# A trunk layer's first projections on unnormed x, with the rows' factor applied behind them

## The chip, the cores and the metric

The kernel runs on one core of one Trainium2 chip. The metric is device time in microseconds, the median of three runs. Five engines work side by side, each in the order in which the program gives it its instructions: TensorE (PE, with its weight loads as PEld), VectorE (DVE), ScalarE (ACT), GpSimd (POOL) and SyncE (SP), which here only issues transfers. An engine waits on semaphores for what another one or a DMA has to deliver; whatever stands behind the waiting instruction on the same engine waits too.

## The reference

One decoder layer on x of 512 rows and 1024 columns, all float32. Only the beginning matters here:

```python
u = rmsnorm(x, ln1_g[i])          # x * rsqrt(mean(x*x) + eps) * g
proj = u @ w_in[i]
q, k, v, pool_in, z, xbc, dt_raw, gate_pre = jnp.split(proj, split_idx, axis=-1)
...
y_a = dilated_attention_mixer(q, k, v, rel_bias) @ w_a[i]
y_b = pool_mixer(pool_in, pool_w[i], pool_scale[i]) @ w_b[i]
y_c = ssd_mixer(z, xbc, dt_raw, ...) @ w_c[i]
...
x = x + merged @ w_o[i]
x = x + conv_ffn(rmsnorm(x, ln2_g[i]), ...)
return rmsnorm(x, final_g)
```

The norm's factor is one number for each row of x; `g` is one for each column. So a projection of `x * g` differs from that of `u` by a factor for each row of the output. `pool_mixer` takes windowed means of 2, 4, 8 and 16 rows of `pool_in`, less `pool_in` itself, and multiplies by small matrices. The attention has three groups of heads, and their values `v` are three stretches of 384 columns.

## The kernel before

**Products in three parts.** A float32 matrix is split in a high part (the value rounded to the fast float32 format of PE) and a low part (what is left). `mm3` (line 230) makes each product from three: high by high, high by low, low by high. So every operand costs a copy to the high part (mostly ACT) and a subtraction for the low one (mostly DVE).

**Jobs.** `program` (line 1709) yields the jobs in order: four jobs for `pool_in` (256 columns each, two PSUM results of 128 columns by 512 rows), two for the first value group (400 columns with `dt_raw`, four K blocks each, four blocks of rows), three for q and k, then `pool_out_job`, and so on. A job's weights are fetched by SP (`fetch`, line 173) to one of two raw buffers, cast to the high part by ACT (`cast`, line 185) and subtracted by DVE to the low part (`low`, line 221). The loop at line 1943 stands ahead of each job's products with the low part of the next job, the cast of the one after and the fetch of the third.

**Small work between.** `step` (line 155) advances what is in `running` and `waiting` by one segment, mostly once for each PSUM result. `after(n, it)` holds a generator back by n steps. The queue of each engine is in program order (`ORDERED`, line 1975), so where `step` is called sets what stands behind what.

**The start.** Lines 1797 to 1939 load x in eight tiles of 128 rows by 512 columns, and `eye` and the gains `g8`. For row blocks 0 and 1 the sums of squares, a root and a few small operations give each row's factor, which goes on the diagonal of `diag`; `turn_scale` (line 1875) multiplies by it, so a transposed and normed block comes out in one product. `turned` (line 1844) applies `g` and splits, 256 columns at a time, to `uh` and `ul`, the transposed normed x in eight blocks of K. Blocks 2 and 3 are scaled in place and transposed (`turns`). `begin` (line 1851) issues the products of the first two jobs in two halves of 256 rows; its last calls evacuate with `pool_evac`. `WARM` products at the start keep PE busy before data is there.

**Pooling.** `pool_evac` (line 890) copies the PSUM result to `pu` on ACT, adds it up in windows on POOL (a doubling sum `psw`: one addition for windows of 2, four for 16, each with a small copy for the first columns), and two steps later DVE and ACT form `pd` and its parts.

**Values and sums.** `v_jobs` (line 621) evacuates by ACT copies to `v0` and `dtr`. `sums_of_u` (line 402) rebuilds u as `uh + ul` in pairs of blocks and makes the sums that `Seven` (line 346), a scheme with seven products in place of eight, needs later. `v_pair` (line 641) makes value groups 1 and 2 that way; its `done` issues the transfers of the rows to their places from SP as soon as the instruction that forms them is written.

**Memory.** Most tiles of 128 by 512 come from one pool of `NBIG` = 52 (`T`, line 106). PSUM has four banks for products (`MM`) and four for small work (`SM`).

Of the kernel before, what the change touches and what calls it, by code (L numbers as in the profile page):

```python
# [82 lines left out]
def trunk(ctx: ExitStack, tc, out, x, rel_bias, ln1_g, w_in, b_gate, w_a, pool_w, pool_scale, w_b,  # L83
# [318 lines left out]
    def sums_of_u(p):  # L402

        f = []
        for k in (2 * p, 2 * p + 1):
            f.append(T("uf"))
            dve.tensor_tensor(f[-1], uh[:, k, :].bitcast(F32), ul[:, k, :].bitcast(F32), OP.add)
# [208 lines left out]
    dtr = cpool.tile([P, 4, SH], F32, name="dtr")  # L616

    both = cpool.tile([P, 4, 32 + HEADS], F32, name="nmls")
    V, QK, OT, NM, LS = {}, {}, {}, {}, {}

    def v_jobs(g):
# [16 lines left out]
        return jobs_b(parts, 384 + extra, lambda k, tb: uh[:, k, tb * P:(tb + 1) * P],  # L638
                      lambda k, tb: ul[:, k, tb * P:(tb + 1) * P], KD, evac)

    def v_pair():
# [9 lines left out]
        def done(hi, right, i, r, ps, op):  # L651
# [10 lines left out]
            for n in range(4):  # L662
                if (g, n) not in V:
                    V[g, n] = T(f"vr{g}")
                sp.dma_start(V[g, n][32 * tb:32 * tb + 32, :384], r[n:P:4, :])
# [224 lines left out]
    def pool_evac(m, ps):  # L890
# [3 lines left out]
        act.copy(u, ps)  # L894
# [814 lines left out]
    def program():  # L1709
        yield from jobs_a(w_in, C_POOL, 8, uhk, ulk, KD, pool_evac)  # L1710
# [103 lines left out]
    first = [MM("pa") for _ in range(4)]  # L1814

    def warm_up(n):
        for i in range(n):
            pe.matmul(first[3][:, :P], ones.bitcast(F32), ones.bitcast(F32), start=True, stop=True)
# [14 lines left out]
    def row_squares(tb, ss, n=1, eng=dve):  # L1833

        for i in range(n):
            squares(act, xin[tb + i, 0], ss[:, i:i + 1])
            squares(eng, xin[tb + i, 1], ss[:, n + i:n + i + 1])
        dve.tensor_tensor(ss[:, :n], ss[:, :n], ss[:, n:2 * n], OP.add)
        return ss[:, :n]

    def x_block(tb, k):
        return xin[tb, k // 4][:, (k % 4) * P:(k % 4 + 1) * P]

    def turned(k, lo, ps):

        hh = uh[:, k, lo:lo + 256]
        act.mul(hh, ps, g1[:, k:k + 1])
        dve.scalar_tensor_tensor(ul[:, k, lo:lo + 256], ps, g1[:, k:k + 1], hh.bitcast(F32),
                                 OP.mult, OP.subtract)

    def begin(n, lo, hi, between=lambda early: None):
        wh, wl = weights[n].split
        js = range(2)
        order = [(wh, uh, k, j) for j in js for k in js]
        for k in range(2, KD + 2):
            order += [(wh, uh, k, j) for j in js if k < KD] + [(wh, ul, k - 2, j) for j in js]
        for part in (order, [(wl, uh, k, j) for j in (1, 0) for k in range(KD)]):
            for a, b, k, j in part:
                pe.matmul(first[2 * n + j][:, lo:hi], a[:, k, j * P:(j + 1) * P], b[:, k, lo:hi],  # L1859
                          start=a is wh and b is uh and k == 0, stop=a is wl and k == KD - 1)  # L1860
            between(part is order)
        if hi == S:
            for j in range(2):
                pool_evac(2 * n + j, first[2 * n + j])
                step()


    warm_up(WARM)
    diag = [T("diag") for _ in range(2)]
    banks = [SM("uT") for _ in range(4)]  # L1870

    def bank(k):
        return banks[k % 4][:, (k // 4) * 256:(k // 4) * 256 + 256]

    def turn_scale(tb, k):
        pe.matmul(bank(k)[:, tb * P:(tb + 1) * P], x_block(tb, k), diag[tb][:, :P], start=True, stop=True)

    for tb in range(2):
        s0, s1, v, sq, r, rt = (small(n, [P, 1]) for n in ("s0", "s1", "v", "sq", "r", "rt"))
        squares(act, xin[tb, 0], s0)  # L1880
        squares(dve, xin[tb, 1], s1)
        dve.tensor_scalar(v, s0, 1.0 / D, EPS, OP.mult, OP.add)
        act.activation(sq, s1, AF.Sqrt, bias=v, scale=1.0 / D)
        dve.scalar_tensor_tensor(rt, s1, 1.0 / D, v, OP.mult, OP.add)
        dve.reciprocal(r, sq)
        dve.scalar_tensor_tensor(rt, r, rt, r, OP.mult, OP.mult)
        dve.tensor_scalar(rt, rt, -0.5, 1.5, OP.mult, OP.add)
        dve.tensor_scalar(diag[tb][:, :P], eye, r, rt, OP.mult, OP.mult)
        if tb == 0:
            for k in range(KD):  # L1890
                turn_scale(0, k)
# [119 lines left out]
```

## Time and profile before

| | us |
|---|---|
| median of 3 runs | 1016.05 (1015.79 to 1016.18) |
| the profiled execution | 1017.29 |
| its span | 1015.5 |
| TensorE busy | 1001.4 |
| mean granted TensorE clock | 0.998 |

Times below are microseconds from the start of the span, unless they are durations. A row of the timeline has start, duration, engine, line, operation, the tile written and the tiles read, the shape and the count; several alike in a row are merged. In brackets stands how long the engine was idle before and what ended it. A row of waits has the engine and line that waited, what it waited for, the sum in us, the number of waits and the longest. The chain of waits follows the work that ended last back from the end and lists its pieces in order of time. A row of a stretch has its length and then busy time and count for PE, PEld, DVE, ACT and POOL, the granted clock, the share of DMA time and GB/s.

### The profile page before, as it was taken

To read this page: it belongs to the slowest core of one execution; us is meant where nothing else is said; L and a number is where in the kernel's file an instruction comes from. 1 tells how busy PE (TensorE), PEld (TensorE's weight loads), DVE (VectorE), ACT (ScalarE), POOL (GpSimd) and SP (SyncE) were. 2 spreads that over 40 slices of the span, in tenths; PEclk is the share of its full clock that TensorE was granted. 3 is DMA by queue.
4 is the path that set the end of the run, shared out by engine and by line. 5 is a ranking of instruction groups with operands and counts; after the bars stand their busy time and mean duration, and the time that the engine had idled before them with its cause. 6 is when DMAs were issued, how large, how long until landed. Compare 5 with 4: busy or idle time off the path is not lost.

```text
span 1015.5 us, 13677 instructions
## 1 busy us (share of the span) xinstructions
PE 1001.4 (99%) x5360; PEld 852.9 (84%) x5360; DVE 734.2 (72%) x932; ACT 527.2 (52%) x895; POOL 154.9 (15%) x142
## 2 busy tenths in 40 slices
PE   8999999999999999999999999999999999999996
PEld 8998878999988888888888887898888888888885
DVE  6564768576767655776879888768778768685877
ACT  5433556453436466788576245554454434443454
POOL 1680010110000000000045501302111100121041
PEclk9999999999999999999999999999999999999999
DMA  8244270653352435552253754232252134542574
GB/s 244 83 107 132 89 203 4 181 159 112 126 165 73 116 95 147 142 130 62 83 150 120 219 187 86 84 122 87 90 200 83 46 115 152 175 115 73 145 183 118
DMA packets 117727, 127.03 MB, mean 125 GB/s; under 512 B 6787, under 2 KB 96454, under 8 KB 117663
## 3 DMA queue, kind: packets, MB, share of 16 engines
q1 hardware_dynamic: 111887, 116.39, 37.1%
q0 software_dynamic: 5184, 8.92, 5.6%
q8 instruction: 42, 0.69, 0.3%
q10 hardware_dynamic: 592, 0.86, 0.3%
q14 instruction: 22, 0.18, 0.1%
HBM read 121.30 MB, written 3.00 MB: 122 GB/s over the span
## 4 chain that ended last, share of the span: by engine, by line
PE 90%; DVE 4%; DMA 2%; issue 2%; ACT 1%; POOL 0%; SPq 0%; ACTq 0%; POOLq 0%; DVEq 0%
PE pa L238 36%; PE pu L238 23%; PE pqk L238 6%; PE pd L238 6%; PE pb L238 6%; PE pq L238 3%; PE pa L1859 2%; DVE wl L217 1%; PE ps L775 1%; PE ppw L238 1%; PE po L823 1%; PE pt L809 1%; PE py L1108 1%; PE pu L1536 1%; DMA w<-in_ffn_w_down_dram 1%
## 5 line engine op out<-in xcount | busy, mean ns | idle before, releaser
L217 DVE TENSOR_TENSOR wl<-raw,wh 128x2048 fp32r<-128x2048 f32 (+3 forms) x86 | 206.1, 2396 | 43.6 <-ACT wh L195 33.9
L195 ACT CAST wh<-raw 128x1024 fp32r<-128x1024 f32 (+3 forms) x169 | 169.8, 1022 | 52.3 <-DVE raw L361 21.3
L1433 DVE SCALAR_TENSOR_TENSOR hc<-pu,fcol,hc 128x510 f32<-128x510 f32 x88 | 65.8, 748 | 53.1 <-ACT hc L1430 51.4
L238 PE MATMUL pa<-uh,wh 128*128 128x512 f32 (+1 forms) x368 | 88.8, 381 | 0.0
L238 PE MATMUL pa<-ul,wh 128*128 128x512 f32 (+1 forms) x368 | 86.8, 375 | 0.0
L238 PE MATMUL pa<-uh,wl 128*128 128x512 f32 (+1 forms) x368 | 86.8, 375 | 0.0
L238 PE MATMUL pu<-uh,wh 128*128 128x512 f32 (+1 forms) x352 | 83.6, 379 | 0.0
L238 PE MATMUL pu<-uh,wl 128*128 128x512 f32 (+1 forms) x352 | 83.5, 379 | 0.0
L238 PE MATMUL pu<-ul,wh 128*128 128x512 f32 (+1 forms) x352 | 83.5, 379 | 0.0
L238 PEld LDWEIGHTS pa<-ul,wh 128*128 128x128 f32 x368 | 66.7, 188 | 12.6
L238 PEld LDWEIGHTS pa<-uh,wl 128*128 128x128 f32 x368 | 66.7, 188 | 12.5
L238 PEld LDWEIGHTS pa<-uh,wh 128*128 128x128 f32 x368 | 65.3, 189 | 11.8
L238 PEld LDWEIGHTS pu<-ul,wh 128*128 128x128 f32 x352 | 64.2, 188 | 12.5
L238 PEld LDWEIGHTS pu<-uh,wl 128*128 128x128 f32 x352 | 64.2, 188 | 12.5
L238 PEld LDWEIGHTS pu<-uh,wh 128*128 128x128 f32 x352 | 64.1, 188 | 12.4
L1438 POOL TENSOR_TENSOR hc<-hc 128x512 f32<-128x512 f32 x22 | 29.9, 1360 | 279.4 <-DVE hc L1433 243.3
L1430 ACT ACTIVATE hc<-pu,fcol,fcol 128x512 f32<-128x512 f32 x40 | 31.2, 779 | 75.0 <-PE pu L238 75.0
L217 DVE TENSOR_TENSOR wl<-w,wh 128x2048 fp32r<-128x2048 f32 (+1 forms) x26 | 55.1, 2118 | 8.9 <-issue 4.6
L195 ACT CAST wh<-w 128x1024 fp32r<-128x1024 f32 (+1 forms) x52 | 47.2, 950 | 10.4 <-DMA w<-in_ffn_w_down_dram 5.7
L797 ACT ACTIVATE sb<-sb,nmls 128x128 f32<-128x128 f32 (+1 forms) x72 | 30.0, 418 | 31.5 <-DVE nmls L794 20.8
L1091 POOL TENSOR_TENSOR st<-st,dts 128x512 f32<-128x512 f32 x4 | 4.2, 1050 | 226.8 <-ACT st L1099 166.6
L1435 ACT ACTIVATE hc<-hc 128x512 f32<-128x512 f32 x22 | 13.9, 632 | 40.3 <-DVE hc L1433 40.3
(436 smaller groups left out, 1964.3 us busy)
## 6 DMA issues: line engine op xcount, KB each, us to landing
raw<-in_w_in_dram SPq DMA_DIRECT2D x24, 1024.0 KB, 5.6
raw<-in_ffn_w_up_dram SPq DMA_DIRECT2D x22, 1024.0 KB, 5.1
raw<-in_w_in_dram SPq DMA_DIRECT2D x14, 512.0 KB
raw<-in_w_in_dram SPq DMA_DIRECT2D x8, 768.0 KB, 7.2
raw<-in_ffn_w_down_dram SPq DMA_DIRECT2D x6, 1024.0 KB, 5.0
raw<-in_w_b_dram SPq DMA_DIRECT2D x4, 1024.0 KB, 5.2
al<-ad SPq DMA_DIRECT2D x16, 256.0 KB, 7.1
raw<-in_w_c_dram SPq DMA_DIRECT2D x4, 1024.0 KB, 7.6
```

What stands on the lines that cost most here:

```text
L195: (other.tensor_copy if other and i else act.copy)(job.high[:, :, o], job.raw[:, :, o])
L217: (eng or dve).tensor_tensor(l[:, :, o], job.raw[:, :, o], h[:, :, o].bitcast(F32), OP.subtract)
L238: pe.matmul(ps, l, r, start=first and n == 0, stop=last and n == total - 1, skip_group_check=onto)
L775: pe.matmul(pss[i][:, o:o + w * P], q[r, n * P:(n + 1) * P], k[r, kb * P:(kb + w) * P], start=True, stop=True)
L797: act.activation(sb[:, off:off + w * P], sb[:, off:off + w * P], AF.Exp, bias=nm[:, n, h:h + 1], accum_out=ls[:, n, h:h + 1])
L809: pe.transpose(pt[:, o:o + P], sb[:, o:o + P], eye)
L823: pe.matmul(po[DH * hh:DH * hh + DH, n * P:(n + 1) * P], V[g, kb + i][:, (2 * c + hh) * DH:(2 * c + hh + 1) * DH], probs[2 * c + hh, nb][: ...
L1430: act.activation(t, ps, AF.Identity, bias=ff["c1"][:, ff["b"] + m:ff["b"] + m + 1], scale=fw(2, m))
L1433: dve.scalar_tensor_tensor(t[:, sh:], ps[:, :S - sh], fw(k, m), t[:, sh:], OP.mult, OP.add)
L1435: act.activation(t, t, AF.Silu)
L1438: pool.tensor_tensor(a, a, t, OP.mult)
L1859: pe.matmul(first[2 * n + j][:, lo:hi], a[:, k, j * P:(j + 1) * P], b[:, k, lo:hi], start=a is wh and b is uh and k == 0, stop=a is wl and ...
```

## The change

The row factor leaves the front. x is transposed as loaded, multiplied by `g` and split to `xh` and `xl` (eight tiles each, blocks of 128 rows at a time). The four pooling jobs and the two jobs of the first value group use those. The first job's products are issued by hand in five pieces; the second job goes through the ordinary loop. The sums of squares follow, and the four factors of each partition (`rcol`) are transposed, stored and read back as a row for every partition (`rows`). `pool_evac` multiplies by that row on DVE; the values' evacuation multiplies by `rcol` on ACT. `xf` holds `x * g` (made by POOL for row blocks 0 and 1, by ACT for 2 and 3); `normed` scales it in the following steps and fills `uh` and `ul`, and `sums_of_u` takes the first four blocks from it. The loads at the start are issued in another order, with `g8` from POOL. In `v_pair` the transfers of value rows become a generator that runs one step later.

```diff
     def sums_of_u(p):
-        f = []
-        for k in (2 * p, 2 * p + 1):
-            f.append(T("uf"))
-            dve.tensor_tensor(f[-1], uh[:, k, :].bitcast(F32), ul[:, k, :].bitcast(F32), OP.add)
+        if p < 2:
+            f = [xf[2 * p], xf[2 * p + 1]]
+        else:
...
+    def normed(k0, k1):
+        for k in range(k0, k1, 2):
+            for i in (k, k + 1):
+                dve.tensor_tensor(xf[i], xf[i], rows["r"], OP.mult)
+                act.copy(uh[:, i, :], xf[i])
+            yield
+            for i in (k, k + 1):
+                dve.tensor_sub(ul[:, i, :], xf[i], uh[:, i, :].bitcast(F32))
...
-            act.copy(t[:, :384], ps[:, :384])
+            act.mul(t[:, :384], ps[:, :384], rcol[:, tb:tb + 1])
             if extra:
-                act.copy(dtr[:, tb, :], ps[:, 384:400])
+                act.mul(dtr[:, tb, :], ps[:, 384:400], rcol[:, tb:tb + 1])
...
-            if g == 2:
-                sp.dma_start(vd[tb * P:(tb + 1) * P, :], r)
+            def store():
+                if g == 2:
+                    sp.dma_start(vd[tb * P:(tb + 1) * P, :], r)
+                    return
+                for n in range(4):
...
+            running.append(after(1, store()))
...
         u = T("pu")
-        act.copy(u, ps)
+        dve.tensor_tensor(u, ps, rows["r"], OP.mult)
...
-        yield from jobs_a(w_in, C_POOL, 8, uhk, ulk, KD, pool_evac)
+        yield from jobs_a(w_in, C_POOL, 8, xhk, xlk, KD, pool_evac)
...
-    load_x(0, (sp, act))
-    act.dma_start(eye, c_eye)
-    load_x(1, (sp, act))
-    act.dma_start(g8[:KD, :P], ln1_g[0].rearrange("(k p) -> k p", p=P))
+    sp.dma_start(eye, c_eye)
+    load_x(0, (act, sp))
+    pool.dma_start(g8[:KD, :P], ln1_g[0].rearrange("(k p) -> k p", p=P))
...
-    fetch(weights[0], 2)
-    fetch(weights[1])
+    load_x(1)
+    load_w0(0, 0, 8)
+    load_w0(1, 0, 8)
     load_x(2)
     load_x(3)
+    fetch(w1)
...
+    def low0(j, k0, k1):
+        o = part(j, k0, k1)
+        pool.tensor_tensor(l0[o], raw0[o], h0[o].bitcast(F32), OP.subtract)
...
+    def split_x(tb, k):
+        c = slice(tb * P, (tb + 1) * P)
+        act.mul(xh[k][:, c], bank(tb, k), g1[:, k:k + 1])
+        dve.scalar_tensor_tensor(xl[k][:, c], bank(tb, k), g1[:, k:k + 1], xh[k][:, c].bitcast(F32),
                                  OP.mult, OP.subtract)
...
     warm_up(WARM)
...
     pe.transpose(first[2][:, :KD], g8[:KD, :P], eye[:KD, :KD])
+    turned(0)
     dve.tensor_copy(g1, first[2][:, :KD])
...
     for k in range(KD):
+        split_x(0, k)
+    turned(1)
+    for k0 in (0, 4):
+        dve.tensor_copy(h0[part(0, k0, k0 + 4)], raw0[part(0, k0, k0 + 4)])
+        low0(0, k0, k0 + 4)
+        for k in range(k0, k0 + 4):
+            split_x(1, k)
+    both_high(0, 256, (0,))
+    for k0 in (0, 4):
+        act.copy(h0[part(1, k0, k0 + 4)], raw0[part(1, k0, k0 + 4)])
+        low0(1, k0, k0 + 4)
+    group(0, (LH,), 0, 256)
+    half_squares(act, 0, 0)
+    half_squares(act, 0, 1)
     for k in range(KD):
+        pool.tensor_tensor(xf[k][:, :256], xh[k][:, :256].bitcast(F32), xl[k][:, :256].bitcast(F32),
+                           OP.add)
+    group(1, (HH,), 0, 256)
+    turned(2)
+    for k in range(KD):
+        split_x(2, k)
+    group(1, (HL,), 0, 256)
+    turned(3)
+    for k in range(KD):
+        split_x(3, k)
+    group(1, (LH,), 0, 256)
+    fetch(weights[2])
+    for tb in (1, 2, 3):
+        half_squares(act, tb, 0)
+        half_squares(dve, tb, 1)
+    cast(w1, 2)
+    both_high(256, S, (0, 1))
+    group(0, (LH,), 256, S)
+    dve.tensor_tensor(ss[:, :4], ss[:, :4], ss[:, 4:], OP.add)
+    r = rstd_of(ss[:, :4], 4, D)
+    dve.tensor_copy(rcol, r)
+    pe.transpose(first[2][:4, :P], rcol, eye)
+    rt, rd = T("rowsT"), dram.tile([S], F32, name="rows")
+    dve.tensor_copy(rt[:4, :P], first[2][:4, :P])
+    rows["r"] = T("rows")
+    sp.dma_start(rd.rearrange("(t p) -> t p", p=P), rt[:4, :P])
+    sp.dma_start(rows["r"], rd.partition_broadcast(P))
+    group(1, (LH,), 256, S)
+    low(w1, 2)
+    for k in range(KD):
+        for tb in (2, 3):
+            act.mul(xf[k][:, tb * P:(tb + 1) * P], bank(tb, k), g1[:, k:k + 1])
     parts_of_bias()
+    cast(weights[2])
     fetch(weights[3])
...
+    running.append(after(3, columns_of(turn)))
+    for j in range(2):
+        pool_evac(j, first[j])
+        step()
+    running.append(normed(0, KD))
...
-        if n >= 2:
+        if n >= 1:
...
-WARM = 12
+WARM = 10
```

`group` issues one part of the first job's products for eight K blocks; `both_high` interleaves the two parts that use the high weights; `turned(tb)` now transposes one block of rows to two PSUM banks.

More of the change, by code (lines that the diff above doesn't have):

```diff
@@ L1851, in begin @@
[L1851 to L1865, printed above, removed]
@@ L1868, in trunk @@
-    warm_up(WARM)
[L1869 to L1891, printed above, removed]
+    h0 = w0.high = whp.tile([P, KD, 256], F32R, name="wh", tag="wh")
@@ new lines, in trunk, with part, turned @@
+    l0 = wlp.tile([P, KD, 256], F32R, name="wl", tag="wl")
+    w0.split = h0, l0
+    def part(j, k0, k1):
+        return slice(None), slice(k0, k1), slice(j * P, (j + 1) * P)
+    def low0(j, k0, k1):
+        o = part(j, k0, k1)
+        pool.tensor_tensor(l0[o], raw0[o], h0[o].bitcast(F32), OP.subtract)
+    banks = {}
+    def turned(tb):
+        for h in range(2):
+            banks[tb, h] = SM("uT")
+            for j in range(4):
+                o = slice(j * P, (j + 1) * P)
+                pe.transpose(banks[tb, h][:, o], xin[tb, h][:, o], eye)
@@ new lines, in group, with both_high, half_squares @@
+    def group(j, pairs, lo, hi, ks=range(KD)):
+        for w, b in pairs:
+            for k in ks:
+                mm(j, w, b, k, lo, hi, w is l0 and k == KD - 1)
+    HH, HL, LH = (h0, xh), (h0, xl), (l0, xh)
+    def both_high(lo, hi, js):
+        for k in range(KD + 1):
+            for w, b, i in ((h0, xh, k), (h0, xl, k - 1)):
+                if 0 <= i < KD:
+                    for j in js:
+                        mm(j, w, b, i, lo, hi)
+    ss = small("ss", [P, 8])
+    def half_squares(eng, tb, h):
+        i = 4 * h + tb
+        squares(eng, xin[tb, h], ss[:, i:i + 1])
@@ L1931, in trunk @@
+    dve.tensor_copy(rt[:4, :P], first[2][:4, :P])
[4 more added lines that the diff above has]
+    low(w1, 2)
+    for k in range(KD):
+        for tb in (2, 3):
+            act.mul(xf[k][:, tb * P:(tb + 1) * P], bank(tb, k), g1[:, k:k + 1])
     parts_of_bias()
[L1932 removed]
+    cast(weights[2])
     fetch(weights[3])
[L1934 to L1935 removed]
```

94 lines of the change are left out of this document (37 added, 57 removed).

## The prediction

> **What bounds the kernel now.** I read the page first, then the table of who waited for whom on PE, then the chain of work for the first 80 us.
>
> ```profile
> span 1015.5 us, 13677 instructions
> PE 1001.4 (99%) x5360; PEld 852.9 (84%) x5360; DVE 734.2 (72%) x932; ACT 527.2 (52%) x895; POOL 154.9 (15%) x142
> ```
> ```profile
> PE uT L1876 <- DVE diag L1888: 2.5, 2, 1.5
> PE pa L1818 <- DVE ones L1809: 1.1, 1, 1.1
> PE pu L1536 <- DVE wl L217: 1.0, 1, 1.0
> PE pb L238 <- ACT wh L195: 0.7, 1, 0.7
> ```
> ```profile
> 10.07 2.05 PE uT L1876 x16
> 12.12 9.59 PE pa L1859 x80
> ...
> 25.50 0.27 PE colp L507
> 25.77 11.54 PE pa L1859 x96
> 37.31 21.79 PE pa L238 x96
> ```
>
> PE is the bound: busy for 1001.4 of 1015.5 us, and its waits add up to little. Only two places can pay: the front before PE's first product (about 12 us), and any new wait later. After 12 us PE runs without a gap, so a delay on another engine costs nothing until it reaches a matmul, and from there it costs in full. The profiled execution took 1017.29 us, 1.24 above the median 1016.05; I work out a difference and apply it to both. A measurement of this kernel can tell about 0.2% (2 us) from no change.
>
> **The front.** Before, x is normed ahead of the transposes, so PE waits for `diag`. After, x is transposed raw, split in blocks of 128 rows, and the row factor comes later. The rows that price this:
>
> ```profile
> 4.69 0.69 DVE L441 SCALAR_TENSOR_TENSOR junk<-xin 128x512 f32<-128x512 f32 x1 [3.48 <-DMA xin<-in_x_dram]
> 10.01 0.68 DVE L195 CAST wh<-raw 128x1024 fp32r<-128x1024 f32 x1
> 10.77 4.76 POOL L217 TENSOR_TENSOR wl<-raw,wh 128x1024 fp32r<-128x1024 f32 x2 [10.32 <-DVE wh L195]
> 10.82 3.27 ACT L1847 ACTIVATE uh<-uT,g 128x256 fp32r<-128x256 f32 x8 [0.89 <-PE uT L1876]
> 11.33 3.39 DVE L1848 SCALAR_TENSOR_TENSOR ul<-uT,g,uh 128x256 fp32r<-128x256 f32 x8 [0.64 <-ACT uh L1847]
> 13.95 2.02 ACT L195 CAST wh<-raw 128x1024 fp32r<-128x1024 f32 x2
> 15.84 0.66 ACT L439 ACTIVATE junk<-xin 128x512 f32<-128x512 f32 x1
> 16.37 0.22 ACT L439 ACTIVATION_READ_ACCUMULATOR junk<-xin 128x1 f32 x1
> 19.74 0.16 DVE L433 TENSOR_TENSOR r<-rt,r 128x2 f32<-128x2 f32 x1
> 21.55 1.91 PE L1925 MATMUL uT<-eye,xin 128*128 128x128 f32 x16
> 29.47 2.08 PE L1859 MATMUL pa<-uh,wl 128*128 128x256 f32 x16
> ```
> ```profile
> w<-in_w_in_dram POOLq DMA_DIRECT2D x8, 192.0 KB, 5.2
> ```
>
> The first x lands by 4.69, so the transposes can start near 4.9. But `g8` now comes over POOL's queue and stands ahead of them on PE. No row shows so small a transfer there; the nearest took 5.2 us from issue. Issued at about 0.5 it lands between 4.7, with x, and 6.2; I take 5.2, and the column of gains is ready at 5.8.
>
> One transpose costs 0.12 (16 in 1.91), where the matmul with `diag` cost 0.26 (8 in 2.05). That saving falls mostly into time in which PE waits anyway. A split of 256 columns has a pitch of 0.40 to 0.42 (8 in 3.27 and 3.39, the last not overlapped); half as wide it lies between 0.20 and 0.42, and I take 0.27. So 16 blocks on DVE, two copies of 0.36 among them, end at 5.8 + 0.7 + 4.3 + 0.9 = 11.7; the first product starts at 9.1, but the stretch that they pace ends at 11.85, before: no earlier than `begin` did in effect. Then PE alone: a group of eight costs 0.96 (0.12 each, 16 in 2.08). Low part, second column's high part, transposes 0.9, group, transposes 0.9, group: 17.5. Thirty-two products: 21.3. One more group: 22.3.
>
> There PE meets the transpose of `rcol`, a **new wait**. ACT splits blocks 2 and 3 from 14.5 to 18.8, does three squares of 0.83 (21.3), and, written ahead of the square root, casts `w1` for 2.0 (23.3). Root and six small DVE operations (0.16, 0.19 with the gap to the next) make it 24.7: PE stands for 2.4 us. The last group ends at 25.8, and the second job follows with 48 products of 512 columns at 0.227 (96 in 21.79): 36.7. With `colp` 0.35 the third job starts at 37.1, against 37.31. **Front: -0.2 us**; with late or early `g8` and pitches 0.20 to 0.33 between -1.5 and +1.6.
>
> The new ACT work (16 scalings of `xf`, eight copies to `uh`) is hidden by ACT's idle half: busy 9.84 of 22 us in the stretch below. If that cover went, casts would be late in the way described next for DVE. The eight evacuations leave ACT.
>
> **The pool stage.** DVE takes over each `pool_evac`, and `normed` adds 16 two-operand operations there. The rows:
>
> ```profile
> 36.00:58.00 22.00, 22.00 (x103) 18.43 (x103) 15.00 (x13) 9.84 (x14) 20.69 (x24) 1.00 0.43 118
> ```
> ```profile
> 34.55 2.29 DVE L217 TENSOR_TENSOR wl<-raw,wh 128x2048 fp32r<-128x2048 f32 x1 [7.03 <-ACT wh L195]
> 40.88 0.76 DVE L910 TENSOR_TENSOR pdl<-pd,pdh 128x512 fp32r<-128x512 f32 x1 [0.69 <-ACT pdh L909]
> 50.78 2.65 DVE L217 TENSOR_TENSOR wl<-raw,wh 128x1600 fp32r<-128x1600 f32 x1
> 53.80 1.51 DVE L907 SCALAR_TENSOR_TENSOR pd<-psw,pu 128x512 f32<-128x512 f32 x1 [0.37 <-POOL psw L901]
> 61.77 1.81 DVE L217 TENSOR_TENSOR wl<-raw,wh 128x1600 fp32r<-128x1600 f32 x1
> 81.40 1.28 DVE L407 TENSOR_TENSOR uf<-uh,ul 128x512 f32<-128x512 f32 x2
> ```
> ```profile
> 33.23 0.19 POOL L899 COPY psw<-pu 128x1 f32<-128x1 f32 x1
> 34.63 2.25 POOL L899 COPY psw<-pu 128x1 f32<-128x1 f32 x1
> 50.39 1.35 POOL L898 TENSOR_TENSOR psw<-psw 128x508 f32<-128x508 f32 x1
> 53.72 1.04 POOL L898 TENSOR_TENSOR psw<-pu 128x511 f32<-128x511 f32 x1
> ```
> ```profile
> 60.40 0.90 PE L238 MATMUL pb<-wl,uh 128*128 128x400 f32 x4
> ```
> ```profile
> L1117 DVE TENSOR_TENSOR ea<-pyo,ea x6: 676/684/693, 405.3 to 484.5; 128x512 f32<-128x512 f32 x6
> ```
> ```profile
> DMA to landing us min/median/max: 1.6/3.6/4.1
> ```
>
> DVE and POOL exclude each other here. POOL's copy of one column takes 0.19 alone and 2.25 beside DVE's 2.29 us `wl`; DVE's `pd` takes 1.51 beside a POOL addition of 1.04; `wl` of 1600 takes 1.81 alone and 2.65 beside POOL. POOL is busy 20.69 of 22 us, so an added DVE operation mostly meets it at the port. The Trainium skill, SBUF — State Buffer, section "SBUF: two separate sides", says that only DVE operations with two SBUF inputs, or in a two-port mode, share a lock with GpSimd, held for the whole instruction. By that rule the evacuations from PSUM escape and `normed` does not; the rows above agree for two inputs, and no row shows a PSUM operation of this kind beside POOL in this stage.
>
> The deadline is the first product with `wl` of the first value job, at 60.4. Before, that `wl` was done at 53.4: 7 us of slack. After, DVE can do no evacuation until the row factors have made their way: `rt` at 25.3, a store of 1.6 and a broadcast of 3.6 (the DMAs of `rdram`, smallest and median), with issues of 0.4 each: 31.3. From there DVE's queue up to that `wl`, in program order:
>
> - six evacuations at 0.65 (0.684 alone, as a product of PSUM and SBUF): 3.9
> - two `wl` at 2.25 and one at 1.8: 6.3
> - four `pd` and four `pdl` at 0.60 (two `uf` in 1.28): 4.8; waits of 0.69 for `pdh` between them: 2.8
> - `normed`: eight products and six subtractions at 0.60: 8.4; `col` 0.2
>
> That is 26.4, to 57.7 without any wait at the port: no stall. The old list, 14.1 of these, took 18.9 (34.55 to 53.43), so 4.8 went to POOL; with those alone it ends at 62.5, a stall of 2.1. If each of the 14 `normed` operations also gives way to one POOL instruction, an addition of 0.97 or a copy of 0.2, mean 0.59, another 8.2: 70.7, a stall of 10.3. POOL also runs dry at times, when its next sum waits for an evacuation. I take 6.0, nearer the upper end because of the row with POOL at 20.69 of 22.
>
> The second value job's `wl` stands behind two evacuations, two `nsub`, two pairs of `pd` and `pdl`: 8.1 us of own work, 11.6 with the port, for some 9.7 us of PE products: 0 to 1.9; I take 1.5, with the value evacuations on ACT behind the last `pdh`. Four `uf` additions (2.4 us of DVE) fall away later, where DVE isn't late: nothing. Sum for the stage: **+7.5 us**, between 0 and +12.
>
> **Value stores.** SP issues the stores one step later, so fetches behind them are no longer held.
>
> ```profile
> SPq L665 <- DVE r L657: 17.3, 1, 17.3
> ```
>
> SP waited 17.3 us in one piece there, yet PE lost only 0.7 in all of that region (`pb` on ACT `wh`). Worth 0 to -0.7; the late value rows are read only by `attend(1)`, a group of jobs later. I take 0. Holding 24 more of the 52 row tiles from the start can tie writers to late readers; no row prices it, and it is in the upper end.
>
> **Sum:** 1017.29 - 0.2 + 7.5 = 1024.6 for the profiled execution; from the median, 1016.05 + 7.3 = **1023.4 us**.
>
> **Rivals.**
> - *DVE keeps pace* (the other side). Place: `wl` of the first value job; price: the 7.5 vanish if POOL's additions slip between DVE's operations, so that it is done before 60.4. For: 57.7 of own work. Against: the 1.51 and 2.65 rows. It gives 1015.9. Chance 0.21.
> - *Keeps pace, and the front gains.* `g8` no later than x and a pitch of 0.24 for 32 blocks bring the front to -1.5, the stores -0.7: 1013.8. Against: the `rcol` wait doesn't shrink with them, for it hangs on ACT's order. Chance 0.09.
> - *The front doesn't come forward at all*: `g8` at 6.2 or later, all behind it +1.6 and the row factors with it: 1025.5. Chance 0.06.
> - *PE loses its clock.* PE's front is now warm-up to about 4.2, transposes, and gaps up to 9.1. Half speed for the first 3.4 us of products would add some 1.3: 1024.7. The row for it: a gap of 1.5 before L1876 cost nothing, two batches alike. The Trainium skill, TensorE: Matmul & The Clock Gate, says in Part 4 that transposes don't count as busy for the gate and in Part 1 that an idle window of about 3.4 us halves the clock; by that rule this front could qualify, and no run here has such a gap. Chance 0.04.
>
> **How the numbers follow.** Forecast 0.60. Slower: 0.60 + 0.06 + 0.04 = 0.70; the same 0.20 (most of the first rival); faster 0.10. The range goes from 1014.8, which takes in the first rival, to 1027.5 (a stall near 10).
>
> **What would show it.** In the after-profile: the first product near 9 us, a PE wait of 2 to 3 us on `rcol` near 22, the third job's start near 37; `evac` on DVE first near 31; POOL still at its sums after 80 us; PE waiting for DVE's `wl` in the first value job for about 6 us and once more shortly after. Wrong would be: no PE wait on `wl` near 60 (DVE not saturated), or one on PSUM slots or casts instead.

## The result, and the profile after

The changed kernel takes 1033.5 us (median of 4 runs, 1033.07 to 1034.01) beside 1015.92 for the kernel before: a ratio of 1.0174, with a 95% interval of 1.0157 to 1.0192. The direction was forecast, but for a part of the kernel that turns out to hold the smaller part of the loss; the time lies 6 us above the range. The profiled execution took 1033.83 us, 16.5 more than that of before.

The page of the changed kernel (span and busy times), then its table of who waited for whom on PE (sum, number, longest):

```profile
span 1032.1 us, 13626 instructions
PE 1009.0 (98%) x5293; PEld 855.2 (83%) x5293; DVE 750.2 (73%) x955; ACT 536.6 (52%) x927; POOL 166.3 (16%) x153
```
```profile
PE pa L1909 <- DVE wh L1941: 4.5, 1, 4.5
PE pa L1974 <- DVE rcol L1973: 2.9, 1, 2.9
PE pa L1909 <- ACT xh L1897: 2.8, 2, 2.5
PE pb L238 <- DVE wl L217: 1.5, 2, 1.2
...
PE pqk L238 <- ACT dtr L661: 0.8, 1, 0.8
```

In the front PE now waits 10.2 us (`wh`, `rcol`, `xh`) where it waited 2.5 for `diag`; on `wl` it waits only 1.5. PE's busy time grew by 7.6 us although it has fewer instructions: some products ran longer. Some of them stand in the 9 us behind the first wait. Eight products of 256 columns in the changed kernel, then in e8 (a run below, in which the clock is whole there):

```profile
20.32 1.91 PE L1909 MATMUL pa<-xh,wh 128*128 128x256 f32 x8
```
```profile
16.59 1.12 PE L1909 MATMUL pa<-xh,wh 128*128 128x256 f32 x8
```

From 12.7 to 22.0 us the granted clock is 0.50; in the kernel before it is 1.00 in this part.

The chain of waits of the changed kernel over the same stretch as before's (start, duration, what):

```profile
12.71 0.55 PE pa L1909
13.28 2.37 PE pa L1909 x6
15.66 6.56 PE pa L1909 x25
...
33.62 1.83 ACT junk L442 x6
35.46 1.88 ACT wh L195 x2
39.33 1.15 DMA rows<-rowsT
40.50 3.13 DMA rows<-rows
```

Two places of the timeline divide the loss: the start of the third job and the start of the query and key jobs. First PE in the changed kernel:

```profile
52.31 2.10 PE L238 MATMUL pa<-xh,wh 128*128 128x512 f32 x8
95.52 2.14 PE L238 MATMUL pqk<-uh,wh 128*128 128x512 f32 x8 [0.84 <-ACT dtr L661]
```

and in the kernel before:

```profile
37.15 2.00 PE L238 MATMUL pa<-uh,wh 128*128 128x512 f32 x8
77.46 1.98 PE L238 MATMUL pqk<-uh,wh 128*128 128x512 f32 x8
```

The third job starts 15.2 us later: that is the **front**. From there to the query and key jobs it is 43.2 us and not 40.3: the **pool stage** adds 2.9. From there to the end it is 936.6 and not 938.0 us. Together 16.7, the difference of the two spans to 0.1 us. (The 1.4 us less at the end is probably no gain: e3 has 936.6 there too and is no faster than the kernel before, whose profiled execution took 1.2 us more than its median.) The forecast had -0.2 and +7.5.

Why the front is late stands in ScalarE's rows at the split of row block 0:

```profile
6.51 0.37 ACT L1897 ACTIVATE xh<-uT,g 128x128 fp32r<-128x128 f32 x1 [3.83 <-PE uT L1890]
7.30 0.37 ACT L1897 ACTIVATE xh<-uT,g 128x128 fp32r<-128x128 f32 x1 [0.42 <-DVE xl L1898]
8.08 0.37 ACT L1897 ACTIVATE xh<-uT,g 128x128 fp32r<-128x128 f32 x1 [0.42 <-DVE xl L1898]
8.87 0.62 ACT L1897 ACTIVATE xh<-uT,g 128x128 fp32r<-128x128 f32 x2 [0.42 <-DVE xl L1898]
```

ACT's high part of block k+1 uses nothing that DVE's low part of block k makes, and yet waits for it, 0.42 us each time. Only at the change from k = 3 to k = 4 (the row "x2") does it go on at once. `bank(tb, k)` puts four neighbouring blocks in one PSUM bank: within a bank the pitch is 0.79 us, across the change 0.25, mean 0.655. The kernel before took its blocks from banks in turn. Each bank holds one tile here, so whether the order is kept by bank or by tile can't be told from these runs.

### The profile page after: what moved, and what is told of

It reads as the page before. It is cut to its first block, busy times and chain, and to the rows that moved or that the text cites. A ratio compares the mean times of both kernels' runs of the same rounds, so it can differ in the third digit from the quotient of the medians.

```text
span 1032.1 us, 13626 instructions
## 1 busy us (share of the span) xinstructions
PE 1009.0 (98%) x5293; PEld 855.2 (83%) x5293; DVE 750.2 (73%) x955; ACT 536.6 (52%) x927; POOL 166.3 (16%) x153
## 4 chain that ended last, share of the span: by engine, by line
PE 89%; DVE 7%; ACT 2%; issue 1%; DMA 0%; ACTq 0%; DVEq 0%
PE pa L238 33%; PE pu L238 22%; PE pb L238 8%; PE pd L238 7%; PE pqk L238 6%; PE pq L238 3%; DVE wl L217 2%; PE ps L806 1%; PE ppw L238 1%; PE po L854 1%; PE pa L1909 1%; PE py L1139 1%; PE pt L840 1%; DVE ul L645 1%; PE pu L1567 1%
## 5 line engine op out<-in xcount | busy, mean ns | idle before, releaser
L217 DVE TENSOR_TENSOR wl<-raw,wh 128x2048 fp32r<-128x2048 f32 (+3 forms) x86 | 206.5, 2402 | 35.1 <-ACT wh L195 25.2
L195 ACT CAST wh<-raw 128x1024 fp32r<-128x1024 f32 (+2 forms) x169 | 169.1, 1017 | 53.2 <-DVE raw L361 17.8
L238 PE MATMUL pa<-uh,wh 128*128 128x512 f32 (+1 forms) x336 | 80.9, 380 | 0.0
L238 PE MATMUL pa<-ul,wh 128*128 128x512 f32 (+1 forms) x336 | 78.9, 374 | 0.0
L238 PE MATMUL pa<-uh,wl 128*128 128x512 f32 (+1 forms) x336 | 78.8, 374 | 0.0
L238 PEld LDWEIGHTS pu<-uh,wh 128*128 128x128 f32 x352 | 64.1, 188 | 12.4
L238 PEld LDWEIGHTS pa<-ul,wh 128*128 128x128 f32 x336 | 60.7, 188 | 11.4
L238 PEld LDWEIGHTS pa<-uh,wl 128*128 128x128 f32 x336 | 60.7, 188 | 11.2
L238 PEld LDWEIGHTS pa<-uh,wh 128*128 128x128 f32 x336 | 59.4, 189 | 10.7
L217 DVE TENSOR_TENSOR wl<-w,wh 128x2048 fp32r<-128x2048 f32 (+1 forms) x26 | 54.2, 2086 | 10.2 <-issue 4.5
L1466 ACT ACTIVATE hc<-hc 128x512 f32<-128x512 f32 x22 | 13.9, 632 | 40.3 <-DVE hc L1464 40.3
```

The costliest lines, as they stand in the source:

```text
L195: (other.tensor_copy if other and i else act.copy)(job.high[:, :, o], job.raw[:, :, o])
L217: (eng or dve).tensor_tensor(l[:, :, o], job.raw[:, :, o], h[:, :, o].bitcast(F32), OP.subtract)
L238: pe.matmul(ps, l, r, start=first and n == 0, stop=last and n == total - 1, skip_group_check=onto)
L1466: act.activation(t, t, AF.Silu)
```

## The experiments

Theory A: the order of the splits within a bank makes the front; a wait of PE then costs clock besides; the pool stage is DVE's and POOL's doing. Theory B, the rival, puts the loss on the order of ACT's and DVE's other work, the transfers, or takes a second effect away. In the texts on record A and B are stated anew for each run.

**e1: the blocks taken from two banks in turn.**

```diff
+    TURNS = (0, 4, 1, 5, 2, 6, 3, 7)
-    for k in range(KD):
+    for k in TURNS:
         split_x(0, k)
```
(and so at the other splits and in `both_high`; DVE's two copies of the first high weights follow one another.)

> The changed kernel with the blocks split in the order 0, 4, 1, 5, 2, 6, 3, 7, so that neighbours in the order lie in two PSUM banks instead of one; the products follow that order, and DVE's second copy of the weights stands right behind the first. Theory A (ACT's scaling of a block waits for DVE's reading of the block before it, because both are in one bank): the rows of the changed kernel have 0.79 us for a block after one of the same bank and 0.25 after one of another bank; alternating, ACT and DVE each need about 0.39 us a block instead of 0.655, 16 blocks twice save 8 us, the third job starts near 44 instead of 52.3, and the time is about 1025. Theory B (a block of 128 columns costs a full handover from ACT to DVE and back, whatever the bank): no change, 1033.5.

1023.89 us (1023.41 to 1025.56), ratio 1.0089 [1.0074, 1.0104]. ACT in e1, ten blocks merged to a row, and PE's third job:

```profile
6.42 3.67 ACT L1897 ACTIVATE xh<-uT,g 128x128 fp32r<-128x128 f32 x10 [3.74 <-PE uT L1890]
```
```profile
42.09 2.10 PE L238 MATMUL pa<-xh,wh 128*128 128x512 f32 x8
```

A block costs 0.37 to 0.39 us, and the third job comes 10.2 us sooner. Each of the two passes of 16 blocks, from ACT's first start to its last end, is 4.5 us shorter (11.2 to 6.7, 10.6 to 6.0); the second of them has no other edit in it. Between the two passes another 1.0 us went, where PE's products lose less clock. So 9.6 of the 17.6 us lost hung on which bank a block lay in; theory A held.

**e2: PE kept busy during its wait for `rcol`**, by ten small products.

```diff
     group(0, (LH,), 256, S)
...
+    warm_up(10)
     pe.transpose(first[2][:4, :P], rcol, eye)
```

> The changed kernel with ten more warm-up products (ones by ones, into a bank that is free there) ahead of the transpose of rcol, in the 2.9 us in which PE stands. Theory A (the wait lets PE's clock drop, and so the first eight products behind it take 3.3 us instead of 1.8): with the wait filled they take 1.8, and the time is 1.5 us less, 1032.0. Theory B (these products are slow for another reason, operands or the weights' arrival): no change, 1033.5, or more if the ten products themselves are late for rcol.

1033.38 us, ratio 1.0178 [1.0161, 1.0195]: nothing gained. The second job's products in the changed kernel, then in e2, then two of e2's waits:

```profile
39.78 3.52 PE L238 MATMUL pa<-xh,wh 128*128 128x512 f32 x8
43.10 2.09 PE L238 MATMUL pa<-xl,wh 128*128 128x512 f32 x8
```
```profile
38.97 2.00 PE L238 MATMUL pa<-xh,wh 128*128 128x512 f32 x8
40.81 1.98 PE L238 MATMUL pa<-xl,wh 128*128 128x512 f32 x8
```
```profile
PE pb L238 <- DVE wl L217: 3.1, 2, 2.9
...
PE pa L1975 <- DVE rcol L1973: 0.8, 1, 0.8
```

From start to start the first eight products take 3.32 us behind the wait of 2.9, and 1.84 where PE had been kept busy: the wait costs clock, 1.5 us. The third job starts 2.4 us sooner. But most of the gain is lost again at `wl`, where PE now stands 2.9 us and not 1.2, and the twelve products behind that wait take 3.8 us from start to start and not 2.3: the query and key jobs start only 0.5 us sooner. So the pool stage had a limit of its own close behind PE.

**e3: the kernel before with the value stores one step later**, the change's last part alone.

```diff
+            running.append(after(1, store()))
```

> The kernel before with only the value rows' transfers issued one step later. Theory A (the change gains here, because a fetch no longer stands behind transfers that wait for their rows): the 0.7 us wait of PE on the cast weights in this region goes, and with it what the second profile shows as 1.4 us less between the start of the value groups and the next group: 1014.6. Theory B (it is hidden): 1016.0.

1015.34 us, ratio 0.9999 [0.9990, 1.0009]. No effect on the time; theory A, which expected 1014.6 us from it, fell. The 0.7 us of PE's wait on cast weights is gone from the trace of e3, as A wanted, but the time of the kernel before, run beside it, is no longer (1015.22 us).

**e4: the changed kernel without POOL's window sums.**

```diff
-        while sh < w:
-            nxt = T("psw")
...
-        pool.tensor_tensor(cur[:, :w], cur[:, :w], ramp[:, g, :w], OP.mult)
```

> The changed kernel without the windowed sums of the pooling on POOL (pd is formed from the evacuated rows themselves, so the pooling branch of the output is another one). Theory A (DVE's queue in the pool stage is stretched by POOL at the shared port): from the first evacuation to the end of the first value job's low weights DVE needs 26 to 28 us instead of 33.3, and PE no longer waits for these weights. Theory B (the added operations alone fill DVE): it stays near 33, and PE waits as before.

1031.88 us in one run (it leaves out the windows of the pooling). DVE's first eviction and its `wl` for the first value job, in the changed kernel and in e4:

```profile
43.65 1.29 DVE L925 TENSOR_TENSOR pu<-pa,rows 128x512 f32<-128x512 f32 x2 [1.28 <-DMA rows<-rows]
...
75.15 1.81 DVE L217 TENSOR_TENSOR wl<-raw,wh 128x1600 fp32r<-128x1600 f32 x1
```
```profile
43.93 1.29 DVE L925 TENSOR_TENSOR pu<-pa,rows 128x512 f32<-128x512 f32 x2 [1.76 <-DMA rows<-rows]
...
69.58 1.82 DVE L217 TENSOR_TENSOR wl<-raw,wh 128x1600 fp32r<-128x1600 f32 x1
```

33.3 us with POOL's sums beside it (43.65 to 76.96), 27.5 without: theory A held. From the third job to the query and key jobs e4 takes 40.4 us (52.09 to 92.50), as the kernel before (40.3).

**e5 to e8: the rest of the front, and the order in the pool stage**, all on e1. e5 begins `normed` four steps later; e6 puts the squares ahead of the splits of row blocks 2 and 3, and the chain to the row factors ahead of the cast of the second job's weights; e7 is both; e8 adds four banks in turn (two row blocks turned first), DVE's weight copies between the splits, and ten small products before the first product.

```diff
-    running.append(normed(0, KD))
+    running.append(after(4, normed(0, KD)))
```
```diff
     half_squares(act, 0, 1)
+    half_squares(act, 1, 0)
+    half_squares(act, 2, 0)
+    half_squares(dve, 1, 1)
...
-    for tb in (1, 2, 3):
-        half_squares(act, tb, 0)
-        half_squares(dve, tb, 1)
...
+    r = rstd_of(ss[:, :4], 4, D)
+    dve.tensor_copy(rcol, r)
     cast(w1, 2)
```
```diff
+    turned(1)
+    warm_up(10)
+    for n, (tb, k) in enumerate(four_banks(0)):
+        split_x(tb, k)
```

> As e1_alternate, and the normalised x (the products by the row factors, their copies and their low parts, 4.2 us of VectorE in each of four steps) begins four steps later, so that it stands behind the low weights of the first value job in VectorE's queue. Theory A (VectorE's queue from the landing of the rows to these low weights, 33.3 us, is what TensorE waits for): the wait of 1.7 us on the low weights and the 0.8 us on the first value rows go, first eviction to low weights takes 21 to 24 us, 1021.4 to 1022.4 us. Theory B (VectorE is full up to the query and key jobs, so a moved step is only late elsewhere): the first query and key job waits for the low part of the normalised x instead, 1023.4 to 1025.

> As e1_alternate, with the squares of row blocks 1 to 3 ahead of the splits of blocks 2 and 3 and the chain to the row factors directly behind the splits, ahead of the cast of the second job's weights; nothing is added. Theory A (squares behind the splits make TensorE wait 2.5 us, and this wait takes its clock for 1.5 us more): the wait falls under 0.5 us, the second job's first eight products take 1.8 to 2.0 us and not 3.3, the third job's first product starts at 37.6 to 38.6 and not 42.1; the rows land about 3 us earlier, a little less than the deadline moves, so the wait for the first value job's low weights grows by about 1: 1020.3 to 1021.5 us. Theory B (as in e2_dummies, whatever the front gains is waited for again at the low weights): the rows do not land earlier, 1023 to 1024.

> e5_normed_later and e6_squares_early together. Theory A: the front gives 4.0, the waits in the pool stage 2.5, and neither is given back: 1016.8 to 1018.2 us. Theory B: one of the two is given back: 1019.5 or above.

> e7_both, with two row blocks turned first and their splits alternated over four PSUM banks (0 and 1, then 2 and 3), VectorE's copies of the first high weights between the splits, and ten small products more so that TensorE keeps its clock before the first product. Theory A (with four banks ScalarE and VectorE do not wait for each other): a block costs 0.26 to 0.30 us and not 0.39 to 0.40, the third job starts at 34 to 36, before the 37.15 of the kernel before; 1013.3 to 1015.0 us, so the change's idea is then no loss at all. Theory B (two readers of a row of banks are ordered whatever the distance, or the copies of the weights set the start): a block stays near 0.39 us, the third job starts at 37 to 38.5, 1016 to 1018.

1025.01, 1024.28, 1025.37 and 1024.41 us; ratios 1.0092 [1.0078, 1.0106], 1.0081 [1.0068, 1.0094], 1.0093 [1.0079, 1.0108] and 1.0088 [1.0075, 1.0102]. By these medians none gained on e1. In the front A held for e6 and nearly for e8; e6, then e8 on ACT and PE:

```profile
27.00 2.00 PE L238 MATMUL pa<-xh,wh 128*128 128x512 f32 x8
37.94 2.10 PE L238 MATMUL pa<-xh,wh 128*128 128x512 f32 x8
64.25 1.00 PE L238 MATMUL pb<-wl,xh 128*128 128x400 f32 x4 [2.81 <-DVE wl L217]
```
```profile
6.48 4.43 ACT L1897 ACTIVATE xh<-uT,g 128x128 fp32r<-128x128 f32 x15 [3.80 <-PE uT L1890]
```
```profile
36.85 2.10 PE L238 MATMUL pa<-xh,wh 128*128 128x512 f32 x8
80.52 3.40 PE L238 MATMUL pqk<-uh,wh 128*128 128x512 f32 x8 [3.10 <-ACT dtr L661]
```

In e6 the clock is whole (eight products in 1.84, start to start) and the third job comes 4.2 us sooner than in e1. In e8 a block costs 0.30 us (15 in 4.43), the third job starts at 36.85, before the one of the kernel before, though not at the 34 to 36 that A wanted. The pool stage takes the gain only in part. It stays 43.3 to 44.8 us long in these four, 3 to 4.5 more than in the kernel before, with a wait each time: in e6 at `wl` (2.8 us), in e5, e7 and e8 at the value rows' eviction (2.7 to 3.5), where ACT's eviction stands behind copies to `uh` that wait for DVE. Behind that wait e8's first eight products again take 3.2 us, start to start (80.52 to 83.76). In the traces, then, a part of the gain is left: the spans of e6, e7 and e8 are 2.8, 1.8 and 3.8 us shorter than that of e1. But these traces are of the fastest run of each kernel; the other runs took 1 to 5 us more at a lower granted clock (e8: 1020.24 us at 0.997 in the trace, 1023.54 to 1025.28 at 0.994 in the others), and no trace shows where. B was right for e5: a moved step is late elsewhere. For e6 its time came true and its reason did not, for the rows landed 2.8 us sooner.

In the changed kernel, e1 and e6, the query and key jobs start 51.9 us after DVE's first eviction (43.65 to 95.52, 33.71 to 85.59, 30.89 to 82.76) and 2.07 after POOL's last sum. That suggested that the landing of the rows sets the end.

**e9 to e12: the rows sooner, or DVE's idle time filled**, on e8. e9 takes the chain to the row factors ahead of the splits of blocks 2 and 3; e10 writes the factors of the pool part as a constant; e11 puts the pooling difference's low part one step behind its high part; e12 is e9 and e11, with DVE's weight copies together.

```diff
+    pool.memset(rows["r"], 1.0)
...
-    sp.dma_start(rd.rearrange("(t p) -> t p", p=P), rt[:4, :P])
-    sp.dma_start(rows["r"], rd.partition_broadcast(P))
```
```diff
             act.copy(dh, d)
+            yield
             dve.tensor_sub(dl, d, dh.bitcast(F32))
```

> As e8_four_banks, with the chain to the row factors and their way through memory ahead of the splits of row blocks 2 and 3 (six of the squares on ScalarE, two on VectorE). In all profiles of changed kernels so far with the pool sums in, VectorE's first eviction and the start of the query and key jobs lie 50.7 to 52.1 us apart, whatever the front does. Theory A (VectorE's queue from the landing of the rows sets the end; TensorE needs only 40.3 us from the third job's start): the first eviction comes at 24.5 to 26 and not 29.8, the third job starts at 36.8 to 38.5, TensorE's waits in the pool stage fall under 1 us, and timed and profiled runs agree: 1015.5 to 1017.5 us. Theory B (the distance is a coincidence, and the value rows' evictions set the end): 1020 to 1024 as e8_four_banks.

> As e8_four_banks, but the row factors of the pool part and of the normalised x are a constant written at the start: it leaves out these factors and their way through memory (the value rows keep theirs). Theory A: the first eviction comes with the end of the first job's products, at 23.5 to 25, and the waits in the pool stage go: 1014.5 to 1016.5 us. Theory B: no change against e8_four_banks, 1020 to 1024.

> As e8_four_banks, and the low part of each pooling difference is issued one step behind its high part, so that VectorE does not stand 0.74 to 0.87 us each for ScalarE's copy (eight times, about 6 us). Theory A: the first eviction stays at 29.8, the distance to the query and key jobs falls from 50.7 to about 45 us, less than TensorE needs, so the waits go: 1015 to 1018 us. Theory B (another instruction on VectorE waits in its place): 1020 to 1024.

> e9_rows_first and e11_pool_spaced together, with VectorE's two copies of the first high weights directly behind one another (1.3 us less wait before the first product). Theory A: TensorE alone sets the end; the third job starts at 35.5 to 37 against 37.15 in the kernel before: 1013.5 to 1016 us. Theory B: 1018 or above.

1021.9, 1021.18, 1022.13 and 1022.73 us; ratios 1.0066 [1.0053, 1.0078], 1.0055 [1.0041, 1.0068], 1.0064 [1.0051, 1.0076] and 1.0072 [1.0059, 1.0084]. Of these only e10 lies clear of e8's interval, and all lie 4 to 7 us above what A wanted. A fell. In e10, where nothing has to land, DVE's first eviction:

```profile
29.09 1.27 DVE L925 TENSOR_TENSOR pu<-pa,rows 128x512 f32<-128x512 f32 x2
```

It starts at 29.1 against 29.8 in e8, without idle time: DVE had other work up to then. In e9 and e12 it starts at 30.5 and 29.0, not at the 24.5 to 26 of A in e9, and again without idle time. So the landing of the rows does not set the end here; what an eviction some us sooner would be worth none of the four shows. PE waits 2.3 to 2.7 us for the value rows' eviction in all four. In e9 and e12 the chain ahead of the splits also costs the front (third job at 40.23 and 40.01).

**e13 to e15: other orders**, on e8: `normed` three or two steps late, and e13 with the two edits of e12 that spare DVE.

```diff
-    running.append(after(4, normed(0, KD)))
+    running.append(after(3, normed(0, KD)))
```

> As e8_four_banks, with the normalised x begun three steps late and not four. Theory A (order): the last copies of the normalised x are done about 8 us sooner on ScalarE, the wait of 3.1 us for the first value rows' eviction falls under 1 us, the low weights of the first value job come at about 57.5 us against the 60.2 at which they are needed, no clock is lost: 1016 to 1018 us. Theory B (the work): the query and key jobs start 42.9 us or more after the third job, 1020 us or more.

> As e8_four_banks, with the normalised x begun two steps late. Theory A: no wait at the value rows' eviction, but the low weights of the first value job stand behind two steps of it and come at about 61.5 us, 1.3 us late: 1017.5 to 1019.5 us. Theory B: 1020 us or more.

> As e13_normed_at_3, with each pooling difference's low part one step behind its high part, and VectorE's two copies of the first high weights behind one another. Theory A: TensorE alone sets the end, the third job starts at 35.5 to 37 us: 1014 to 1016.5 us. Theory B: 1019 us or more.

1023.89, 1021.73 and 1022.9 us; ratios 1.0073 [1.0057, 1.0089], 1.0054 [1.0040, 1.0068], 1.0065 [1.0052, 1.0078]. The longest waits of e13, then of e14:

```profile
PE pqk L238 <- ACT dtr L661: 3.7, 1, 3.7
```
```profile
PE pb L238 <- DVE wl L217: 4.0, 2, 3.7
```

One step of difference moves the same 3.7 us from one place to the other. B held, none of these orders takes the wait away, and the candidate e15 beats neither e14 nor the kernel before. One of e14's six runs took 1018.68 us, inside what A wanted; the other five took 1021.59 to 1022.77.

**e16 and e17: which work it is**, on e8. e16 leaves out the window sums as e4 did; e17 leaves out DVE's eight products of `xf` by the row factors, and so the factors of the normed x.

```diff
-                dve.tensor_tensor(xf[i], xf[i], rows["r"], OP.mult)
```

> As e8_four_banks without GpSimd's window sums (it leaves out the windows of the pooling; the difference is taken from the block itself). Theory A (the sums beside VectorE's work cost the pool stage its 3 us and its clock): the query and key jobs start 40.3 to 40.6 us after the third job and the time is that of the kernel before, 1014.5 to 1016.5 us, with a granted clock of 0.997 or more in every run. Theory B (VectorE's own addition is enough): 2 us of wait or more remain, 1018 us or more.

> As e8_four_banks without VectorE's eight products of x by the row factors (it leaves the factors out of the normalised x), 8.5 us of VectorE less; the sums stay. Theory A: GpSimd's sums still end last and are waited for: 1.5 us of wait or more, 1018 us or more. Theory B: the waits go, 1014.5 to 1017 us.

1016.6 us (ratio 1.0008 [0.9999, 1.0017]) and 1017.43 (1.0018 [1.0009, 1.0027]). The pool stage as one stretch, from the third job to the query and key jobs, in the kernel before, the changed one, e8, e16 and e17 (length, then busy time of PE, PEld, DVE, ACT, POOL):

```profile
37.15:77.46 40.31, 40.31 (x203) 36.04 (x202) 24.88 (x22) 17.15 (x28) 33.60 (x43) 1.00 0.42 114
```
```profile
52.31:95.52 43.21, 41.07 (x202) 35.77 (x200) 35.69 (x41) 15.34 (x25) 34.31 (x40) 1.00 0.28 75
```
```profile
36.85:80.52 43.67, 40.57 (x202) 35.95 (x201) 36.20 (x41) 15.49 (x25) 35.80 (x42) 0.99 0.31 83
```
```profile
38.01:78.42 40.41, 40.41 (x203) 36.12 (x201) 29.34 (x40) 16.62 (x27) 0.00 (x0) 1.00 0.38 95
```
```profile
36.71:77.10 40.39, 40.39 (x203) 36.12 (x201) 32.05 (x33) 15.74 (x27) 34.87 (x42) 1.00 0.35 92
```

DVE is busy 24.9 of 40.3 us before and 35.7 of 43.2 after, while POOL stays at 34. Neither is full, but each waits for the other and for ACT: in this stretch of the changed kernel DVE waits 5.2 us for ACT's `pdh` and 2.2 for POOL's sums, and POOL 5.1 for DVE's evictions. Either removal ends PE's waits in this stage and brings the stage back to 40.4. So the sums are needed for the loss (A of e16), and DVE's products are needed too (B of e17): it takes both. A removal takes out the work and the waits that hang on it at once, and the two are not told apart. In e16 the spread went too: its eleven runs lie between 1015.04 and 1016.82 us at 0.996 to 0.998. e17's lie between 1015.15 and 1018.36 at 0.996 to 0.999, and about 2 us of loss is left in its median.

## Why the prediction was wrong, step by step

- **Front, -0.2: wrong, +15.2.** The step that failed is the pitch of the splits: "half as wide it lies between 0.20 and 0.42, and I take 0.27". It was 0.655 us. The bounds came from splits of 256 columns whose neighbours lay in different banks; the code shows that four new neighbours share one, and I did not ask what two readers of one bank do. The Trainium skill, PSUM — Partial Sum Buffer, section "PSUM bank collisions raise a hardware error", had the rule: engines that touch one bank have to be kept apart by semaphores, by bank and not by address, reads included. The rows agree: 0.79 us within a bank, 0.39 in two banks in turn, 0.30 in four. The two passes of 16 blocks pushed the last group, forecast to end at 25.8, to 39.78. Of the 15.2 us, e1 gave back 10.2 by the order of the banks, e6 another 4.2 by the order of the squares, with the wait and the clock behind it; 0.8 is left.
- **The new wait on `rcol`, 2.4: right, 2.9.** What it costs besides was not in the forecast: the second job ran 1.5 us longer at a lower clock. Its cause was as forecast: the cast and the squares stand ahead of the root on ACT.
- **The rival "PE loses its clock" (0.04, +1.3)** came true beside it, at its own place and about at its price, behind the wait of 4.5 us for `wh`. The sixteen products from 18.61 to 22.02 took 3.4 us, where e8's take 0.95 for eight: 1.5 us more, and they pass on, since ACT's first split of row block 2 waits 3.0 us for the transposes behind them. (Half speed over its 3.4 us of products would have been 1.7, not 1.3.) The second job paid another 1.5.
- **`g8`, 5.2: right.** It was there by 5.62, when PE turned it; the first split started at 6.51 as worked out.
- **The first product, 9.1: late, 12.71**, for DVE's copy of the weights stands behind its eight `xl`: the pitch again.
- **The landing of the rows**: store and broadcast took 1.15 and 3.13 against 1.6 and 3.6, but started at 39.33.
- **DVE's queue up to `wl`, 35.1 (31.3 to 66.4): nearly right, 33.3.** Without POOL it was 26.4 in the forecast and 27.5 in e4; POOL's share was 8.7 in the forecast and is 5.8.
- **The stall, 6.0 and 1.5: too big, 1.2 and 0.3** (the kernel before has the 0.3 too), with 0.8 at `pqk`. The queue was priced well, but PE, too, came 15 us late, and the rows only 12.4 late (43.65 against 31.3). That takes 3.0 from the stall of 6.0, and the shorter queue another 1.8. (6.0 was the middle of the bounds 2.1 and 10.3, not nearer the upper one.) In e6, with the front mended, the stall was 2.8, near half of the forecast.
- **Value stores, 0: right** (e3).
- **The end of the sums after 80 us: right**, 93.45.

So the second mechanism stood, and "slower" would have been right by it alone, but here it made up 2.9 of the 16.7 us. With a front as forecast it would have cost about 6 to 9 us, as an estimate from the kernels on e8 that leave nothing out: they take 1021.7 to 1024.4 us, with the third job at 36 to 40, but in another order of work than the change has. The largest part of the rest is the pitch within a bank. Against that, no order tried here makes the change a gain: with the front 0.3 us ahead of the kernel before (e8) it is still 0.9% slower by its median.

One thing stays open. Runs of one kernel differ more than those of the kernel before, and go with the granted clock: e13 took 1021.4 and 1021.7 us at 0.996, and 1023.4 to 1024.9 at 0.992 and 0.993. Waits near 3 us that sometimes cost the clock would do that, but where the runs that left no trace lose it isn't shown. The part from the query and key jobs to the end, 936.3 to 939.1 us in the changed kernel and e1 to e17, goes with that clock, too. Its first 24 products take 5.44 us with a whole clock; without what they take beyond that behind their wait, all of these lie between 936.1 and 936.8 us.

## What to carry to other kernels

Before pricing a chain in which two engines read PSUM, write down the bank of every tile and look for neighbours in one bank; taking the tiles from two banks in turn was worth 9.6 us here. When PE is 99% busy, price each new wait with the clock behind it. And where two engines share the work of a stage, try a gain in front of it against that stage first: whatever the front gained (e1, e2, e6, e8), the stage behind it stayed 3 us or more too long while DVE had its added products and POOL's sums beside it.

## What the runs showed of the hardware

- The clock can fall after waits shorter than 3 us, and does not after each: behind waits of 2.35 (e12), 2.61 (e11) and 2.9 us (changed kernel) the next eight products of 512 columns took 3.2 to 3.5 us in place of 1.84 (granted clock 0.53 from 39.7 to 43.1 us in the changed kernel); behind waits of 2.70 us in e5 and e9 they took 1.9 to 2.0. Two rows each of e11 and of e9:

```profile
81.06 3.67 PE L238 MATMUL pqk<-uh,wh 128*128 128x512 f32 x8 [2.61 <-ACT dtr L661]
84.56 2.00 PE L238 MATMUL pqk<-ul,wh 128*128 128x512 f32 x8
```
```profile
83.47 2.11 PE L238 MATMUL pqk<-uh,wh 128*128 128x512 f32 x8 [2.70 <-ACT dtr L661]
85.43 2.04 PE L238 MATMUL pqk<-ul,wh 128*128 128x512 f32 x8
```

  The Trainium skill, TensorE: Matmul & The Clock Gate, Part 1, says that the gate's window runs freely, so that its effect depends on where in it the products fall. These rows agree with that, but the waits are shorter than the window of 3.4 us that it names.
- A product of PSUM and SBUF on DVE isn't held up by POOL in these rows, one of two SBUF tiles is. The changed kernel's DVE and, in the third and the last row, POOL:

```profile
58.27 1.28 DVE L641 TENSOR_TENSOR xf<-xf,rows 128x512 f32<-128x512 f32 x2
64.33 2.12 DVE L641 TENSOR_TENSOR xf<-xf,rows 128x512 f32<-128x512 f32 x2
64.53 1.38 POOL L929 TENSOR_TENSOR psw<-psw 128x510 f32<-128x510 f32 x1
81.58 0.68 DVE L925 TENSOR_TENSOR pu<-pa,rows 128x512 f32<-128x512 f32 x1
81.78 1.03 POOL L929 TENSOR_TENSOR psw<-psw 128x508 f32<-128x508 f32 x1
```

  The products take 0.64 while POOL stands idle (58.41 to 62.44) and 1.06 beside its addition, which takes 1.38; the eviction beside an addition takes 0.68, as at 61.69, where POOL is idle, and that addition 1.03. The rows agree with the rule of the Trainium skill, SBUF — State Buffer, section "SBUF: two separate sides", that the prediction had named without a row for the evictions.
